# Grouped softmax on one core: ScalarE sums the last three tiles while it exponentiates them

## The chip, the cores and the metric

The kernel runs on one core of a Trainium2 chip. The metric is the device time of one execution in microseconds; lower is better. The kernel before takes 1326.22 us, the median of four runs (1325.66 to 1326.57).

## The reference

The input `x` is `[4, 4096, 4352]` in float32. Each row of 4352 numbers is cut into 8 groups of 544, and a softmax is taken over each group:

```python
x_g = x.reshape(B, N, G, Dg)                      # G = 8, Dg = 544
x_g = x_g - x_g.max(axis=-1, keepdims=True)
exp = np.exp(x_g)
out = exp / exp.sum(axis=-1, keepdims=True)
```

That makes 131,072 groups. 285.2 MB are read from HBM and as many written.

## The kernel before, in words

**Tiles.** The groups are seen as one list, and each of the 128 SBUF partitions works on 1024 of them. The list is cut into 57 tiles (`sizes`, line 34): 5, 11 and 15 groups per partition, then 51 tiles of `T = 19`, then 10, 9 and 5. A tile of 19 groups is 128 x 10336 floats, 5168 KB. Five buffers (`NT`) take turns: tile `t` lies in `xt` number `t % 5`. The last three tiles have `t` = 54, 55 and 56.

**The quick path.** The maximum is not subtracted. For each tile ScalarE takes the exponential in place, in one instruction for up to 19 groups (`scalar_tile`, line 88; tiles other than those of 19 groups are cut by `parts`, line 49, into pieces of at most `C = 10` groups). VectorE then sums each group (`reduce_sum`, line 102), takes the reciprocals (line 106) and multiplies the tile by them in place (line 109). `exp_done` counts ScalarE's pieces, `sum_done` and `rec_done` order VectorE's own steps, and `scaled` rises by one when a whole tile has been multiplied.

**The check and the slow path.** After the last tile `judge` (line 115) takes the largest and smallest of all sums on VectorE, tests them against 1e30 and 1e-6, adds up the answers over the partitions with a matmul, and writes a `verdict`. SP, ScalarE and VectorE load it (line 160) and branch. Only if a sum was out of bounds do they enter the loop from line 168, which computes everything again with the maximum subtracted. With this input they don't.

**Who moves the data.** SP issues all loads in order (line 137), each after the store that freed its buffer has landed. POOL issues the stores of all tiles but the last two (line 144). SP issues the stores of the last two tiles (line 140, `LAST = 2`), behind its loads. A store is issued when `scaled` has reached its tile. The profile calls SP's transfers q1 (hardware_dynamic) and POOL's q0 (software_dynamic); both run on the same 16 DMA engines.

**How the kernel ends.** The order in which POOL's queue ends is written out by hand:

```python
for t in range(nt - NT, nt - LAST):
    nc.gpsimd.wait_ge(stored[t % NT], 16 * (t // NT + 1))
nc.gpsimd.drain()
nc.gpsimd.wait_ge(last_stored, 16 * LAST)
```

POOL waits until its own last three stores, up to the 10-group tile, have landed. It then drains, waits until SP's two stores have landed, and goes on to the closing barrier of all engines.

Of the kernel before, what the change touches and what calls it, by code (L numbers as in the profile page):

```python
# [9 lines left out]
def kernel(  # L10
# [5 lines left out]
    nc = tc.nc  # L16
    G = 8
    P = 128
    NT = 5
    LAST = 2  # L20
    C = 10
    LOW, HIGH = 1e-6, 1e30
    f32 = mybir.dt.float32
    X = mybir.AxisListType.X
    Exp = mybir.ActivationFunctionType.Exp
    ET = mybir.EngineType
    op = mybir.AluOpType
# [3 lines left out]
    Dg = D // G  # L31
    per = N * G // P
    T = 19
    sizes = [5, 11, 15] + [T] * (per // T - 2) + [10, 9, 5]
    assert sum(sizes) == per
    nt = len(sizes)
    start = [sum(sizes[:t]) for t in range(nt + 1)]
# [9 lines left out]
        return a[lo:hi, :].rearrange("(p g) d -> p (g d)", p=P)  # L47

    def parts(t):
        size = T if sizes[t] == T else C  # L50
        return [(c, min(c + size, sizes[t])) for c in range(0, sizes[t], size)]

    before = [0]
    for t in range(nt):
        before.append(before[-1] + len(parts(t)))

    landed = [tc.alloc_semaphore(f"landed{b}") for b in range(NT)]
    stored = [tc.alloc_semaphore(f"stored{b}") for b in range(NT)]
    last_stored = tc.alloc_semaphore("last_stored")
    exp_done = tc.alloc_semaphore("exp_done")  # L60
    sum_done = tc.alloc_semaphore("sum_done")
    rec_done = tc.alloc_semaphore("rec_done")
    scaled = tc.alloc_semaphore("scaled")
    tested = tc.alloc_semaphore("tested")
# [4 lines left out]
    ctx.enter_context(tc.tile_critical(  # L69
        sync_engine=mybir.EngineType.Pool, no_gpsimd_drain=True))  # L70
    bufs = [ctx.enter_context(nc.sbuf_tensor(f"xt{b}", [P, T * Dg], f32)) for b in range(NT)]
    sums = ctx.enter_context(nc.sbuf_tensor("sums", [P, per], f32))
    rs = ctx.enter_context(nc.sbuf_tensor("rs", [P, NT, T], f32))
    mx = ctx.enter_context(nc.sbuf_tensor("mx", [P, R * G], f32))
    one = ctx.enter_context(nc.sbuf_tensor("one", [P, 1], f32))
    extreme = ctx.enter_context(nc.sbuf_tensor("extreme", [P, 2], f32))
    within = ctx.enter_context(nc.sbuf_tensor("within", [P, 2], f32))
    count = ctx.enter_context(nc.sbuf_tensor("count", [1, 1], f32))
    verdict = ctx.enter_context(nc.sbuf_tensor("verdict", [1, 1], mybir.dt.int32))
    found = ctx.enter_context(nc.psum_tensor("found", [1, 2], f32))  # L80

    def groups(b, lo, hi):
        return bufs[b][:, lo * Dg:hi * Dg].rearrange("p (g d) -> p g d", d=Dg)
# [4 lines left out]
    def scalar_tile(t):  # L88
        b = t % NT
        for k, (lo, hi) in enumerate(parts(t)):  # L90
            i = nc.scalar.activation(  # L91
                out=groups(b, lo, hi), in_=groups(b, lo, hi), func=Exp, scale=1.0)
            if k == 0:
                i.wait_op(landed[b], 16 * (t // NT + 1), "sem-ge")
            i.then_inc(exp_done, 1)

    def vector_tile(t):
        b = t % NT
        size = sizes[t]
        at = start[t]  # L100
        for k, (lo, hi) in enumerate(parts(t)):
            i = nc.vector.reduce_sum(  # L102
                out=sums[:, at + lo:at + hi], in_=groups(b, lo, hi), axis=X).wait_op(
                exp_done, before[t] + k + 1, "sem-ge")
        i.then_inc(sum_done, 1)
        nc.vector.reciprocal(out=rs[:, b, :size], in_=sums[:, at:at + size]).wait_op(  # L106
            sum_done, t + 1, "sem-ge").then_inc(rec_done, 1)
        xg = groups(b, 0, size)
        nc.vector.tensor_tensor(  # L109
            out=xg, in0=xg,  # L110
            in1=rs[:, b, :size].unsqueeze(2).to_broadcast([P, size, Dg]),
            op=op.mult,
        ).wait_op(rec_done, t + 1, "sem-ge").then_inc(scaled, 1)

    def judge():
        nc.vector.memset(one[:, :], 1.0).then_inc(tested, 1)  # L116
        for k, o in enumerate((op.max, op.min)):
            nc.vector.tensor_reduce(  # L118
                out=extreme[:, k:k + 1], in_=sums[:, :], axis=X, op=o).then_inc(tested, 1)
        nc.vector.wait_ge(tested, 3)  # L120
        for k, (o, limit) in enumerate(((op.is_le, HIGH), (op.is_ge, LOW))):
            nc.vector.tensor_scalar(  # L122
                out=within[:, k:k + 1], in0=extreme[:, k:k + 1], scalar1=limit, scalar2=None,
                op0=o).then_inc(tested, 1)
        nc.tensor.wait_ge(tested, 5)
        nc.tensor.matmul(  # L126
            out=found[:, :], lhsT=one[:, :], rhs=within[:, :],
            start=True, stop=True).then_inc(counted, 1)
        nc.vector.wait_ge(counted, 1)
        nc.vector.reduce_sum(out=count[:, :], in_=found[:, :], axis=X).then_inc(tested, 1)  # L130
        nc.vector.wait_ge(tested, 6)
        nc.vector.tensor_copy(out=verdict[:, :], in_=count[:, :]).then_inc(judged, 1)  # L132

    for t in range(nt):
# [16 lines left out]
    for t in range(nt):  # L151
        scalar_tile(t)

    for t in range(nt):
        vector_tile(t)
    judge()

    regs = nc.alloc_registers("verdict", [ET.SP, ET.Activation, ET.DVE])
    for e, reg in zip((nc.sync, nc.scalar, nc.vector), regs):
        e.reg_load(reg, verdict[0:1, 0:1]).wait_op(judged, 1, "sem-ge")  # L160
    with nc.If_cmp(regs, 2 * P, "IS_LT"):
        for t in range(nt - NT, nt - LAST):
            nc.sync.wait_ge(stored[t % NT], 16 * (t // NT + 1))
        nc.sync.wait_ge(last_stored, 16 * LAST)
        xb = bufs[0][:, :R * D]
        xg = groups(0, 0, R * G)
        sm, rg = sums[:, :R * G], rs[:, 0, :R * G]
        with nc.Fori(0, rows, engines=[ET.SP, ET.Activation, ET.DVE]) as t:
            nc.sync.dma_start(
                out=xb, in_=xr[bass.ds(t, 1)].rearrange("t p f -> (t p) f")).then_inc(again["in"], 16)  # L170
            nc.sync.wait_ge(again["out"], 1)
            nc.sync.sem_inc(again["out"], -1)
            nc.sync.dma_start(
                out=outr[bass.ds(t, 1)].rearrange("t p f -> (t p) f"), in_=xb).then_inc(again["end"], 16)
            nc.sync.wait_ge(again["end"], 16)
            nc.sync.sem_inc(again["end"], -16)

            nc.scalar.wait_ge(again["max"], 1)
            nc.scalar.sem_inc(again["max"], -1)
            for g in range(R * G):  # L180
                i = nc.scalar.activation(
                    out=xg[:, g, :], in_=xg[:, g, :], func=Exp,
                    bias=mx[:, g:g + 1], scale=1.0, accum_out=sm[:, g:g + 1])
            i.then_inc(again["exp"], 1)

            nc.vector.wait_ge(again["in"], 16)
            nc.vector.sem_inc(again["in"], -16)
            nc.vector.reduce_max(out=mx[:, :], in_=xg, axis=X, negate=True).then_inc(again["max"], 1)
            nc.vector.wait_ge(again["exp"], 1)
            nc.vector.sem_inc(again["exp"], -1)  # L190
            nc.vector.reciprocal(out=rg, in_=sm).then_inc(again["rec"], 1)
            nc.vector.wait_ge(again["rec"], 1)
            nc.vector.sem_inc(again["rec"], -1)
            nc.vector.tensor_tensor(
                out=xg, in0=xg, in1=rg.unsqueeze(2).to_broadcast([P, R * G, Dg]),
                op=op.mult).then_inc(again["out"], 1)
# [30 lines left out]
```

## Time and profile before

| | |
|---|---|
| median of four runs | 1326.22 us (1325.66 to 1326.57) |
| the profiled execution | 1326.17 us, with a span of 1324.4 us |
| VectorE busy | 1196.0 us (90%) |
| ScalarE busy | 477.3 us (36%) |
| DMA, mean over the span | 431 GB/s |
| exponential of 19 groups, ScalarE | 8.82 us |
| sums of 19 groups, VectorE | 10.92 us |
| multiply of 19 groups, VectorE | 10.93 us |
| start of one 19-group tile to the next, late in the run | 24.5 us |

The span is the time from the first to the last instruction of the core; some 1.8 us of the execution lie around it. The page of the profile gives the busy time of the engines first, then the busy share in 40 slices of 33.1 us each, then the DMA queues, then the chain of work that ended last, and then the groups of instructions by line with the mean time of one and the idle time ahead of them. Semaphore waits, branches and drains are not counted as busy; they are asked for by their line. Windows give the same busy times for any stretch, with the share of the 16 DMA engines that were busy and the GB/s as the last two columns.

### The profile page before, as it was taken

Reading aid. Unit: us, or ns where it says so; the run is one execution under the profiler, and the core shown is the slowest. Engines: PE = TensorE matmul, PEld = TensorE weight load, DVE = VectorE, ACT = ScalarE, POOL = GpSimd, SP = SyncE. Lnnn points to the kernel's source line nnn. Section 1 sums busy time; section 2 is a strip of 40 time slices with the busy share of each in tenths; the row PEclk is TensorE's granted clock in tenths of the full one; section 3 lists DMA queues with packets and bytes.
Section 4 is the critical chain, followed back from the end, with each engine's and each line's share of the span. In section 5 each row is a group of like instructions: output and inputs, shape, how many; then the busy total and the mean of one; then the engine's idle time right before and its main releaser. Section 6 shows DMA issues by size and latency. Waiting matters only on the chain.

```text
span 1324.4 us, 429 instructions
## 1 busy us (share of the span) xinstructions
PE 0.2 (0%) x2; PEld 0.1 (0%) x2; DVE 1196.0 (90%) x180; ACT 477.3 (36%) x60; POOL 29.6 (2%) x59
## 2 busy tenths in 40 slices
PE   0000000000000000000000000000000000000000
PEld 0000000000000000000000000000000000000000
DVE  6999899899899899898898998998998998989998
ACT  4342523423423324325225234234243243252331
POOL 0000000000000000000000000000000000000000
DMA  9999999999999999999999999999999999999998
GB/s 403 422 436 436 428 435 440 430 430 440 431 428 440 437 428 433 438 428 432 440 432 431 436 437 430 432 438 430 431 438 436 430 433 438 428 433 438 430 426 368
DMA packets 16421, 570.47 MB, mean 431 GB/s; under 512 B 1824, under 2 KB 1824, under 8 KB 1824
## 3 DMA queue, kind: packets, MB, share of 16 engines
q1 hardware_dynamic: 8496, 289.12, 50.6%
q0 software_dynamic: 7920, 281.32, 49.1%
q14 instruction: 5, 0.04, 0.0%
HBM read 285.21 MB, written 285.21 MB: 431 GB/s over the span
## 4 chain that ended last, share of the span: by engine, by line
another core or an unknown queue 56%; ACT 33%; DMA 6%; DVE 4%; issue 0%; PE 0%; POOLq 0%; SPq 0%
ACT xt L91 33%; DMA xt<-in_x_dram 4%; DVE xt L109 2%; DVE sums L102 2%; DMA out_dram<-xt 1%; DVE extreme L118 0%; DVE rs L106 0%; DVE within L122 0%; PE found L126 0%; DVE count L130 0%; DVE verdict L132 0%; SPq L222 0%; POOLq L69 0%; POOLq L211 0%
## 5 line engine op out<-in xcount | busy, mean ns | idle before, releaser
L91 ACT ACTIVATE xt<-xt 128x10336 f32<-128x10336 f32 (+4 forms) x59 | 476.0, 8071 | 827.9 <-DMA xt<-in_x_dram 827.9
L102 DVE TENSOR_REDUCE sums<-xt 128x19 f32<-128x10336 f32 (+4 forms) x59 | 589.1, 9987 | 119.2 <-ACT xt L91 119.2
L109 DVE TENSOR_TENSOR xt<-xt,rs 128x10336 f32<-128x10336 f32 (+5 forms) x57 | 589.3, 10339 | 2.0
L144 POOL DMA_DIRECT2D out_dram<-xt x55 | 29.4, 534 | 1270.5 <-DVE xt L109 1270.5
L106 DVE RECIPROCAL rs<-sums 128x19 f32<-128x19 f32 (+5 forms) x57 | 15.4, 270 | 2.0
L118 DVE TENSOR_REDUCE extreme<-sums 128x1 f32<-128x1024 f32 x2 | 2.3, 1214 | 0.0
L150 ACT ACT_TABLE_LOAD x1 | 1.3, 1283 | 0.9 <-PEq L211 0.9
L130 DVE TENSOR_REDUCE count<-found 1x1 f32<-1x2 f32 x1 | 0.1, 148 | 0.3 <-PE found L126 0.3
L126 PE MATMUL found<-within,one 128*1 128x2 f32 x2 | 0.2, 164 | 1318.9 <-DVE within L122 1318.9
L122 DVE TENSOR_SCALAR within<-extreme 128x1 f32<-128x1 f32 x2 | 0.2, 148 | 0.0
L132 DVE CAST verdict<-count 1x1 int32<-1x1 f32 x1 | 0.1, 142 | 0.0
L126 PEld LDWEIGHTS found<-within,one 128*1 128x1 f32 x2 | 0.1, 80 | 1318.9 <-DVE within L122 1318.9
L211 POOL MEMSET const-float32-0.0<- 128x1 f32 x1 | 0.1, 99 | 0.3 <-issue 0.3
L211 POOL MEMSET const-bfloat16-1.0<- 128x1 bf16 x1 | 0.1, 102 | 0.0
L211 POOL MEMSET const-float32-1.0<- 128x1 f32 x1 | 0.1, 99 | 0.0
L211 POOL MEMSET const-uint8-127<- 128x1 uint8 x1 | 0.1, 99 | 0.0
L116 DVE MEMSET one<- 128x1 f32 x1 | 0.1, 59 | 0.0
## 6 DMA issues: line engine op xcount, KB each, us to landing
xt<-in_x_dram SPq DMA_DIRECT2D x51, 5168.0 KB, 55.0
out_dram<-xt POOLq DMA_DIRECT2D x51, 5168.0 KB, 35.8
xt<-in_x_dram SPq DMA_DIRECT2D x1, 4080.0 KB, 23.5
out_dram<-xt POOLq DMA_DIRECT2D x1, 4080.0 KB, 27.8
xt<-in_x_dram SPq DMA_DIRECT2D x1, 2992.0 KB, 12.6
out_dram<-xt POOLq DMA_DIRECT2D x1, 2992.0 KB, 23.5
xt<-in_x_dram SPq DMA_DIRECT2D x2, 1360.0 KB, 19.5
xt<-in_x_dram SPq DMA_DIRECT2D x1, 2720.0 KB, 49.2
```

Of the source, the lines that this page charges most:

```text
L91: i = nc.scalar.activation(out=groups(b, lo, hi), in_=groups(b, lo, hi), func=Exp, scale=1.0)
L102: i = nc.vector.reduce_sum(out=sums[:, at + lo:at + hi], in_=groups(b, lo, hi), axis=X).wait_op(exp_done, before[t] + k + 1, "sem-ge")
L106: nc.vector.reciprocal(out=rs[:, b, :size], in_=sums[:, at:at + size]).wait_op(sum_done, t + 1, "sem-ge").then_inc(rec_done, 1)
L109: nc.vector.tensor_tensor(out=xg, in0=xg, in1=rs[:, b, :size].unsqueeze(2).to_broadcast([P, size, Dg]), op=op.mult,).wait_op(rec_done, t + ...
L116: nc.vector.memset(one[:, :], 1.0).then_inc(tested, 1)
L118: nc.vector.tensor_reduce(out=extreme[:, k:k + 1], in_=sums[:, :], axis=X, op=o).then_inc(tested, 1)
L122: nc.vector.tensor_scalar(out=within[:, k:k + 1], in0=extreme[:, k:k + 1], scalar1=limit, scalar2=None, op0=o).then_inc(tested, 1)
L126: nc.tensor.matmul(out=found[:, :], lhsT=one[:, :], rhs=within[:, :], start=True, stop=True).then_inc(counted, 1)
L130: nc.vector.reduce_sum(out=count[:, :], in_=found[:, :], axis=X).then_inc(tested, 1)
L144: nc.gpsimd.dma_start(out=dram(og_all, t), in_=buf(t)).then_inc(stored[t % NT], 16)
L150: nc.scalar.preload_act_table(Exp)
L211: nc = _bacc.Bacc("TRN2", target_bir_lowering=False, num_devices=1)
```

## The change

For the last three tiles (`SUMMED = 3`) ScalarE issues one exponential for each group, and each of them also writes the sum of its group (`accum_out`) into a new buffer `tail_sums`. These tiles are cut into parts of five groups (`FINE`): 5 + 5, 5 + 4 and 5. `exp_done` rises once for each part. VectorE no longer sums these tiles. For each part it waits for ScalarE's part, takes the reciprocals and multiplies. `scaled` still rises once for each tile, after its last part. Since the sums now lie in two buffers, `judge` takes four extremes instead of two, and tests them two at a time. All other tiles, the loads and the stores are written as before.

```diff
+    FINE = 5
...
+    SUMMED = 3
...
     def parts(t):
-        size = T if sizes[t] == T else C
+        size = FINE if t >= nt - SUMMED else T if sizes[t] == T else C
...
-            i = nc.scalar.activation(
-                out=groups(b, lo, hi), in_=groups(b, lo, hi), func=Exp, scale=1.0)
+            xg = groups(b, lo, hi)
+            if t < nt - SUMMED:
+                runs = [nc.scalar.activation(out=xg, in_=xg, func=Exp, scale=1.0)]
+            else:
+                runs = [
+                    nc.scalar.activation(
+                        out=xg[:, g - lo, :], in_=xg[:, g - lo, :], func=Exp, scale=1.0,
+                        accum_out=tail_sums[:, start[t] - summed + g:start[t] - summed + g + 1])
+                    for g in range(lo, hi)]
             if k == 0:
-                i.wait_op(landed[b], 16 * (t // NT + 1), "sem-ge")
-            i.then_inc(exp_done, 1)
+                runs[0].wait_op(landed[b], 16 * (t // NT + 1), "sem-ge")
+            runs[-1].then_inc(exp_done, 1)
...
+        for k, (lo, hi) in enumerate(whole if t < nt - SUMMED else parts(t)):
+            n = t + 1 if t < nt - SUMMED else nt - SUMMED + before[t] - before[nt - SUMMED] + k + 1
+            from_ = sums if t < nt - SUMMED else tail_sums
+            first = at if t < nt - SUMMED else at - summed
+            i = nc.vector.reciprocal(out=rs[:, b, lo:hi], in_=from_[:, first + lo:first + hi])
+            if t < nt - SUMMED:
+                i.wait_op(sum_done, n, "sem-ge")
+            else:
+                i.wait_op(exp_done, before[t] + k + 1, "sem-ge")
+            i.then_inc(rec_done, 1)
+            xg = groups(b, lo, hi)
+            i = nc.vector.tensor_tensor(
+                out=xg, in0=xg,
+                in1=rs[:, b, lo:hi].unsqueeze(2).to_broadcast([P, hi - lo, Dg]),
+                op=op.mult,
+            ).wait_op(rec_done, n, "sem-ge")
+        i.then_inc(scaled, 1)
...
+        for h, part in enumerate((sums, tail_sums)):
+            for k, o in enumerate((op.max, op.min)):
+                nc.vector.tensor_reduce(
+                    out=extreme[:, 2 * k + h:2 * k + h + 1], in_=part[:, :], axis=X,
+                    op=o).then_inc(tested, 1)
...
-    with nc.If_cmp(regs, 2 * P, "IS_LT"):
+    with nc.If_cmp(regs, 4 * P, "IS_LT"):
```

More of the change, by code (lines that the diff above doesn't have):

```diff
@@ L71 @@
     bufs = [ctx.enter_context(nc.sbuf_tensor(f"xt{b}", [P, T * Dg], f32)) for b in range(NT)]
-    sums = ctx.enter_context(nc.sbuf_tensor("sums", [P, per], f32))
+    summed = start[nt - SUMMED]
+    tail_sums = ctx.enter_context(nc.sbuf_tensor("tail_sums", [P, per - summed], f32))
+    sums = ctx.enter_context(nc.sbuf_tensor("sums", [P, summed], f32))
     rs = ctx.enter_context(nc.sbuf_tensor("rs", [P, NT, T], f32))
@@ L75 @@
     one = ctx.enter_context(nc.sbuf_tensor("one", [P, 1], f32))
-    extreme = ctx.enter_context(nc.sbuf_tensor("extreme", [P, 2], f32))
-    within = ctx.enter_context(nc.sbuf_tensor("within", [P, 2], f32))
+    extreme = ctx.enter_context(nc.sbuf_tensor("extreme", [P, 4], f32))
+    within = ctx.enter_context(nc.sbuf_tensor("within", [P, 4], f32))
     count = ctx.enter_context(nc.sbuf_tensor("count", [1, 1], f32))
     verdict = ctx.enter_context(nc.sbuf_tensor("verdict", [1, 1], mybir.dt.int32))
-    found = ctx.enter_context(nc.psum_tensor("found", [1, 2], f32))
+    found = ctx.enter_context(nc.psum_tensor("found", [1, 4], f32))
     def groups(b, lo, hi):
@@ L100, in vector_tile @@
         at = start[t]
[L101 to L113, printed above, removed]
+        whole = [(0, size)]
@@ new lines, in vector_tile @@
+        if t < nt - SUMMED:
+            for k, (lo, hi) in enumerate(parts(t)):
+                i = nc.vector.reduce_sum(
+                    out=sums[:, at + lo:at + hi], in_=groups(b, lo, hi), axis=X).wait_op(
+                    exp_done, before[t] + k + 1, "sem-ge")
+            i.then_inc(sum_done, 1)
+        for k, (lo, hi) in enumerate(whole if t < nt - SUMMED else parts(t)):
[3 more added lines that the diff above has]
+            i = nc.vector.reciprocal(out=rs[:, b, lo:hi], in_=from_[:, first + lo:first + hi])
+            if t < nt - SUMMED:
+                i.wait_op(sum_done, n, "sem-ge")
[8 more added lines that the diff above has]
+            ).wait_op(rec_done, n, "sem-ge")
@@ L115, in judge @@
+        i.then_inc(scaled, 1)
     def judge():
         nc.vector.memset(one[:, :], 1.0).then_inc(tested, 1)
[L117 to L120, printed above, removed]
+        for h, part in enumerate((sums, tail_sums)):
[3 more added lines that the diff above has]
+                    op=o).then_inc(tested, 1)
@@ L121, in judge @@
+        nc.vector.wait_ge(tested, 5)
         for k, (o, limit) in enumerate(((op.is_le, HIGH), (op.is_ge, LOW))):
             nc.vector.tensor_scalar(
-                out=within[:, k:k + 1], in0=extreme[:, k:k + 1], scalar1=limit, scalar2=None,
-                op0=o).then_inc(tested, 1)
-        nc.tensor.wait_ge(tested, 5)
+                out=within[:, 2 * k:2 * k + 2], in0=extreme[:, 2 * k:2 * k + 2],
+                scalar1=limit, scalar2=None, op0=o).then_inc(tested, 1)
+        nc.tensor.wait_ge(tested, 7)
@@ L130, in judge @@
         nc.vector.reduce_sum(out=count[:, :], in_=found[:, :], axis=X).then_inc(tested, 1)
-        nc.vector.wait_ge(tested, 6)
+        nc.vector.wait_ge(tested, 8)
         nc.vector.tensor_copy(out=verdict[:, :], in_=count[:, :]).then_inc(judged, 1)
```

## The prediction

> **What bounds the kernel now.** I read the page first, then the DMA windows of the last 16 us, then the timeline of the end, and last the sequencer instructions of the end. Call the last three tiles A (10 groups), B (9) and C (5), and the 19-group tile before them T.
>
> ```profile
> span 1324.4 us, 429 instructions
> PE 0.2 (0%) x2; PEld 0.1 (0%) x2; DVE 1196.0 (90%) x180; ACT 477.3 (36%) x60; POOL 29.6 (2%) x59
> DMA  9999999999999999999999999999999999999998
> q1 hardware_dynamic: 8496, 289.12, 50.6%
> q0 software_dynamic: 7920, 281.32, 49.1%
> ```
>
> VectorE is busy 90%, but the DMA row is at 9 in all slices but the last, and the two queues fill 99.7% of sixteen engines' span. q1 carries the loads and the stores of B and C (SP), q0 all other stores (POOL). VectorE's 90% is the second limit, not the first.
>
> ```profile
> 1306.00:1308.00 2.00, 0.00 (x0) 0.00 (x0) 2.00 (x1) 0.13 (x1) 0.00 (x0) 1.00 0.99 424
> 1308.00:1310.00 2.00, 0.00 (x0) 0.00 (x0) 2.00 (x1) 0.00 (x0) 0.00 (x0) 1.00 1.04 446
> 1310.00:1312.00 2.00, 0.00 (x0) 0.00 (x0) 2.00 (x2) 0.00 (x0) 0.00 (x0) 1.00 0.80 337
> 1312.00:1314.00 2.00, 0.00 (x0) 0.00 (x0) 1.93 (x3) 0.00 (x0) 0.00 (x0) 1.00 0.74 313
> 1314.00:1316.00 2.00, 0.00 (x0) 0.00 (x0) 2.00 (x1) 0.00 (x0) 0.00 (x0) 1.00 1.09 470
> 1316.00:1318.00 2.00, 0.00 (x0) 0.00 (x0) 2.00 (x4) 0.00 (x0) 0.00 (x0) 1.00 0.80 339
> 1318.00:1320.00 2.00, 0.19 (x2) 0.09 (x2) 1.13 (x5) 0.00 (x0) 0.00 (x0) 1.00 1.02 430
> ```
>
> The last two columns are the DMA share and GB/s. VectorE works almost without a pause to 1319.5 us and the chain of waits runs along it, which suggests that each microsecond off VectorE is a microsecond gained. But the DMA engines starve only a little: the unfilled shares of these rows, the two above 1 counted against them, come to 2 x (0.20 + 0.26 + 0.20 - 0.09 - 0.02 - 0.04 + 0.01) = 1.0 us. That is nearly all that earlier stores can win back.
>
> ```profile
> 1299.80 0.53 POOL L144 DMA_DIRECT2D out_dram<-xt  x1 [11.31 <-DVE xt L109]
> 1303.66 2.47 ACT L91 ACTIVATE xt<-xt 128x2720 f32<-128x2720 f32 x1 [8.55 <-DMA xt<-in_x_dram]
> 1310.24 6.49 SPq L140 DMA_DIRECT2D out_dram<-xt  x2
> 1313.36 2.99 DVE L109 TENSOR_TENSOR xt<-xt,rs 128x2720 f32<-128x2720 f32 x1
> ```
>
> POOL issues A's store at 1299.80, SP B's at 1310.24 and C's at 1316.38; C's data landed at 1303.6. The issue table gives 13.4, 8.8 and 6.3 us to landing: A lands at 1313.2, B at 1319.0, C at 1322.7.
>
> ```profile
> L147 POOLq DRAIN  x1: 4552/4552/4552, 1313.3 to 1313.3; - x1
> ...
> L137 POOLq COMPARE_BRANCH  x1: 33/33/33, 1322.7 to 1322.7; - x1
> ```
>
> These are POOL's last steps: once A's store, the last on its own queue, has landed, it drains for 4.55 us (1313.31 to 1317.86), then waits for C's landing, branches at 1322.69, and 1.7 us of closing barriers follow. Today the drain ends 4.8 us before it is needed.
>
> I also read the trace's packet records one by one. Packets of 41,344 B (T) take 1.53 us on an engine, 21,760 B (A) 0.81, 19,584 B (B) 0.73, 10,880 B (C) 0.41. One of the sixteen engines is late. It runs without a gap from 1292 to 1321.86, while the others starve briefly at 1311 and 1317 and still end at 1320.6. C's store lands on fifteen engines at 1320.9 to 1321.0 and on the late one at 1322.67. Each landing counts when the sixteenth is in, so the late engine alone sets the end, and its work doesn't shrink.
>
> **What the Trainium skill says.** "DMA: Bandwidth & Descriptors", section "Queues, rings and completion order": an engine takes turns between the queues that have work, a packet at a time. The records agree: from 1292 to 1302 the late engine alternates one T store packet (1.53 us) with one C load packet (0.41 us). The same page, "Latency and other measured facts", says that some DMA engines are usually slower; the trace has one, 1.7 us late at the end. "PSUM — Partial Sum Buffer", section "Engine vs sequencer instructions": a drain waits for its engine to go fully idle. It gives no price; the trace has 4.55 us. "ScalarE: Activation LUTs", section "What ACT_TABLE_LOAD costs": 186 ns plus 0.833 ns per element, 93 ns less back to back; the 128x544 ACTIVATE took 640 ns and the 128x10336 one 8817, which agrees.
>
> **The change, part by part.**
>
> *ScalarE.* 24 one-group ACTIVATEs with sums replace three large ones (4.74 + 4.28 + 2.47 us). No row has a summing ACTIVATE, and the pages price none. Lower end 0.55 us (640 ns less the overlap), upper 0.95 (640 ns and as much again as a small VectorE instruction, 0.19 to 0.28, for reading out the sum). I take 0.75. A: 1275.3 + 7.5 = 1282.8, hidden under VectorE's work on T until 1287.6. B landed at 1290.8: first five groups at 1294.6, all at 1297.6. C landed at 1303.65: 1307.4.
>
> *VectorE.* Reductions of 5.81 + 5.24 + 2.98 = 14.0 us go; each part costs a reciprocal (0.22 with its gap) and a multiply (2.99 for five groups, about 2.4 for four). A: 1287.6 + 2 x 3.2 = 1294.05, before 1299.5. B: 1294.6 + 3.2 = 1297.8, then 2.6 more, 1300.45, before 1310.2. C: 1307.45 + 3.2 = 1310.65, before 1316.35. The new wait of part two on ScalarE (at most 0.2 us at 0.75 per group) has only that tile's multiply behind it. At 0.95 C ends at 1311.65, still early.
>
> *The verdict.* Two short reductions more, 0.15 to 0.3 us each by the small rows: about 0.4. It is done near 1314.2 instead of 1319.5, and its loads (0.86 us) and branches near 1315.1. POOL's later end hides it; without that cover it would still have C's transfer over it. The branches cause 8 KB instruction fetches (today at 1321.6 and 1321.9, 0.37 to 0.49 us), which would now run under the stores: nothing, or 0.4 us if one meets the late engine. Semaphore and buffer edits cost nothing: no instruction is added to SP or POOL.
>
> *The stores.* A's issue moves to 1294.3, B's to 1300.5, C's to 1310.7. A only joins the queue behind T, which is unchanged. B and C are on q1, which had been empty while A was written. Now B's packets take turns with T's and A's. On the late engine, from 1301.8: q0 still has three T packets (4.6) and eight of A (6.5), 11.1 us. Ten turns of q1 fall between the eleven: the load's semaphore (nothing), B's eight (5.8) and one of C (0.4). One more C packet goes ahead of A's semaphore write. A is written at 1301.8 + 11.1 + 6.2 + 0.4 = 1319.5 instead of 1312.8. C still ends at 1321.9, since the sum of the bytes is the same.
>
> *POOL.* A lands 0.4 later, 1319.9; 0.12 to the drain's start, as before; plus 4.55: 1324.57; the branch at 1324.6 instead of 1322.69. So the end goes 1.9 us **later**: a wait on A through the drain takes the place of the wait on C. The drain's cost is the term that the trace shows only once. Lower end 0.2 us (the longest other POOL drain is 0.18), upper 5; I take 4.55, since POOL had nothing running when it began, so what it paid looks fixed.
>
> **The sum.** The profiled run took 1326.17 us (span 1324.4, 1.8 around it), 0.05 below the median of 1326.22. 1326.17 + 1.9 = 1328.1 us, 0.14% above the median. About 0.2% (2.65 us) is what a measurement of this kernel can tell from no change; I forecast a small loss inside it. With a fetch on the late engine and with a different order of turns around A, it is 1327.3 to 1329.0.
>
> **Rivals.**
> 1. *The drain is not in the way* (it is shorter when the core is quiet: VectorE's multiply ran from 1313.36 to 1316.35 beside it, and if that held it up, 1.5 us remain). Then it ends by 1321.6 and C's landing sets the end as today: 1326.1. For it: the drain shows up once, beside that multiply. Against it: it outlasts the multiply by 1.5 us, and does not end with any VectorE instruction.
> 2. *VectorE's gain arrives*: the late engine is not late in an ordinary run, the 1.0 us of holes closes, and the drain is covered: 1325.1. For it: the chain of waits runs along VectorE. Against it: that engine's unbroken row. More than this isn't there to be won, whatever VectorE saves.
> 3. *Slower beyond 0.2%*: q1 gets more than every other turn, so that A's packets come last with C's. A lands at 1322.3, the drain ends at 1326.95, the branch moves by 4.3: 1330.5. It decides from a landing of A after 1320.6, 0.7 us beyond my estimate. For it: C's packets are short, and a fetch adds 0.4. Against it: the one-to-one turns of 1292 to 1302.
>
> **Chances.** Forecast 0.64 (of which 0.06 over the 0.2% line), rival 1 0.18, rival 2 0.08, rival 3 0.10. Slower by over 0.2%: 0.10 + 0.06 = 0.16; faster by over 0.2%: 0.03, out of rival 2 if holes before 1306 closed too; within: 0.81. The range runs from below rival 1 to the upper end of the forecast, 1325.6 to 1329.2, and leaves out rival 3 and most of rival 2.
>
> **What would show it.** VectorE's last multiply ends near 1310.7 and B's store is issued near 1300.5; ACTIVATE rows of 544 near 0.75 us. A's store takes about 25 us to landing instead of 13.4. The drain starts near 1320 and the branch follows its end directly. The forecast is wrong if the drain takes well under 4 us, if A lands before 1318, or if C's landing is still what POOL waits for last.

## The result, and the profile after

The changed kernel takes 1328.74 us (median of 38 runs), the kernel before 1326.05 us in runs beside it (58 runs). The ratio is 1.0020, with a 95% interval of 1.0015 to 1.0025: slower by 2.0 to 3.3 us. The profiled execution took 1329.40 us, its span is 1327.6 us; before they were 1326.17 and 1324.4.

The top of the page of the changed kernel:

```profile
span 1327.6 us, 477 instructions
PE 0.2 (0%) x2; PEld 0.1 (0%) x2; DVE 1182.7 (89%) x183; ACT 481.5 (36%) x105; POOL 29.7 (2%) x59
DMA  9999999999999999999999999999999999999997
```

VectorE did lose 13.3 us of work, and the span is 3.2 us longer all the same. The DMA row is full as before, except for its last slice, which went from 8 to 7: the end now has more time in which no data move. The timeline of the changed kernel at the end:

```profile
1294.50 0.53 POOL L168 DMA_DIRECT2D out_dram<-xt  x1 [5.72 <-DVE xt L130]
...
1300.27 10.74 SPq L164 DMA_DIRECT2D out_dram<-xt  x2
1304.09 0.66 ACT L100 ACTIVATE xt<-xt 128x544 f32<-128x544 f32 x1 [7.09 <-DMA xt<-in_x_dram]
...
1307.65 2.99 DVE L130 TENSOR_TENSOR xt<-xt,rs 128x2720 f32<-128x2720 f32 x1
```

The stores are early: A's is issued at 1294.5 (before 1299.8), B's at 1300.27 (1310.24), C's at 1310.67 (1316.38). Now the transfers from 1285 us on, with the time from issue to landing as the last column:

```profile
out_dram<-xt POOLq DMA_DIRECT2D x1, 5168.0 KB, 20.4
out_dram<-xt POOLq DMA_DIRECT2D x1, 2720.0 KB, 26.7
out_dram<-xt SPq DMA_DIRECT2D x1, 2448.0 KB, 17.7
out_dram<-xt SPq DMA_DIRECT2D x1, 1360.0 KB, 12.7
```

The last three in the kernel before:

```profile
out_dram<-xt POOLq DMA_DIRECT2D x1, 2720.0 KB, 13.4
out_dram<-xt SPq DMA_DIRECT2D x1, 2448.0 KB, 8.8
out_dram<-xt SPq DMA_DIRECT2D x1, 1360.0 KB, 6.3
```

Each takes twice as long as before, because they now share the engines. A is issued 5.3 us earlier and lands at 1321.2, 8.0 us **later** than before. B lands at 1317.9 (1.1 earlier), C at 1323.4 (0.7 later). POOL's last steps in the changed kernel:

```profile
L171 POOLq DRAIN  x1: 4552/4552/4552, 1321.3 to 1321.3; - x1
```

```profile
L161 POOLq COMPARE_BRANCH  x1: 33/33/33, 1325.9 to 1325.9; - x1
```

The drain runs from 1321.32 to 1325.87 and the branch follows at 1325.92, 2.5 us after the last data landed. Before, the same branch stood at 1322.69, right behind C's landing. The difference of the two, 3.2 us, is the whole difference of the spans. The windows say the same from the side of the DMA engines (share and GB/s are the last two columns):

```profile
1318.00:1320.00 2.00, 0.00 (x0) 0.00 (x0) 0.00 (x0) 0.00 (x0) 0.00 (x0) 1.00 0.66 275
1320.00:1322.00 2.00, 0.00 (x0) 0.00 (x0) 0.00 (x0) 0.00 (x0) 0.00 (x0) 1.00 0.07 27
1322.00:1324.00 2.00, 0.00 (x0) 0.00 (x0) 0.00 (x0) 0.00 (x0) 0.00 (x0) 1.00 0.03 11
```

Fourteen engines have done their share of the last store by 1320.1, one by 1321.0 and the late one by 1323.4. From 1320 on nearly nothing moves, and the kernel lasts 7 us more.

### The profile page after: what moved, and what is told of

Its sections match the earlier page's. It is cut to its first block, busy times and chain, and to the rows that moved or that the text cites. A ratio compares the mean times of both kernels' runs of the same rounds, so it can differ in the third digit from the quotient of the medians.

```text
span 1327.6 us, 477 instructions
## 1 busy us (share of the span) xinstructions
PE 0.2 (0%) x2; PEld 0.1 (0%) x2; DVE 1182.7 (89%) x183; ACT 481.5 (36%) x105; POOL 29.7 (2%) x59
## 4 chain that ended last, share of the span: by engine, by line
another core or an unknown queue 54%; ACT 32%; DMA 10%; DVE 3%; issue 0%; PE 0%; POOLq 0%; SPq 0%
ACT xt L97 31%; DMA xt<-in_x_dram 7%; DMA out_dram<-xt 4%; DVE xt L130 1%; DVE sums L115 1%; ACT xt L100 0%; DVE extreme L141 0%; DVE rs L123 0%; DVE within L146 0%; PE found L150 0%; DVE count L154 0%; DVE verdict L156 0%; SPq L246 0%; POOLq L71 0%
## 5 line engine op out<-in xcount | busy, mean ns | idle before, releaser
L97 ACT ACTIVATE xt<-xt 128x10336 f32<-128x10336 f32 (+3 forms) x56 | 464.5, 8298 | 799.0 <-DMA xt<-in_x_dram 799.0
L115 DVE TENSOR_REDUCE sums<-xt 128x19 f32<-128x10336 f32 (+3 forms) x56 | 575.1, 10272 | 119.5 <-ACT xt L97 119.5
L130 DVE TENSOR_TENSOR xt<-xt,rs 128x10336 f32<-128x10336 f32 (+4 forms) x59 | 589.6, 9994 | 2.0
L100 ACT ACTIVATE xt<-xt 128x544 f32<-128x544 f32 x24 | 15.4, 644 | 26.0 <-DMA xt<-in_x_dram 26.0
L123 DVE RECIPROCAL rs<-sums 128x19 f32<-128x19 f32 (+3 forms) x54 | 14.8, 273 | 1.8
L100 ACT ACTIVATION_READ_ACCUMULATOR xt<-xt 128x1 f32 x24 | 4.5, 189 | 0.0
```

The source lines that it names most:

```text
L97: runs = [nc.scalar.activation(out=xg, in_=xg, func=Exp, scale=1.0)]
L100: nc.scalar.activation(out=xg[:, g - lo, :], in_=xg[:, g - lo, :], func=Exp, scale=1.0, accum_out=tail_sums[:, start[t] - summed + g:start ...
L115: i = nc.vector.reduce_sum(out=sums[:, at + lo:at + hi], in_=groups(b, lo, hi), axis=X).wait_op(exp_done, before[t] + k + 1, "sem-ge")
L123: i = nc.vector.reciprocal(out=rs[:, b, lo:hi], in_=from_[:, first + lo:first + hi])
L130: i = nc.vector.tensor_tensor(out=xg, in0=xg, in1=rs[:, b, lo:hi].unsqueeze(2).to_broadcast([P, hi - lo, Dg]), op=op.mult,).wait_op(rec_do ...
```

## The experiments

The theory is "drain behind A": the earlier store of B slows A's store down, and the drain, which stands behind the wait for A, ends after the last landing. Rival "instructions": the added instructions or the longer check cost the time. Rival "transfers": stores that share the engines land later as a whole. Each measured ratio is against the kernel before on the same chip, with its 95% interval.

### The instructions without the order: b_held

```diff
     for t in range(nt - LAST, nt):
-        nc.sync.wait_ge(scaled, t + 1)
+        nc.sync.wait_ge(scaled, nt)
```

> The changed kernel, but SP issues B's store only when C has been multiplied too, near 1310.7, so that A has the engines to itself as before. Drain behind A: A lands near 1313 to 1314, the drain is over by 1318.5, 1326.1 us with all of the changed computation kept. Transfers: also 1326.1, since the stores no longer mix. Instructions: 1328.7.

Measured: 1326.35 us, ratio 1.0000 (0.9992 to 1.0009). B's and C's stores are issued at 1308.6 and 1309.0 (C had loaded 2 us sooner than in the changed kernel), A lands at 1313.9, the drain is over at 1318.5, and the branch waits for C's landing at 1322.84:

```profile
L171 POOLq DRAIN  x1: 4552/4552/4552, 1314.0 to 1314.0; - x1
```

```profile
L161 POOLq COMPARE_BRANCH  x1: 33/33/33, 1322.9 to 1322.9; - x1
```

All of the changed computation is there and the loss is gone. The rival "instructions" falls.

### The order without the instructions: before_no_tail_sums2

```diff
-        for k, (lo, hi) in enumerate(parts(t)):
-            i = nc.vector.reduce_sum(
...
+        if t < nt - 3:
+            for k, (lo, hi) in enumerate(parts(t)):
+                i = nc.vector.reduce_sum(
...
+        else:
+            nc.vector.reciprocal(out=rs[:, b, :size], in_=sums[:, :size]).wait_op(
+                exp_done, before[t + 1], "sem-ge").then_inc(rec_done, 1)
```

The extremes are taken over the sums that are still written.

> The kernel before, which leaves out the sums of the last three tiles and scales these by the reciprocals of the first tiles' sums instead: VectorE is as early as in the changed kernel, with nothing added on ScalarE and the small check as before. Drain behind A: B is issued near 1300.6, A lands near 1321, 1328.7 us. Instructions (the summing ACTIVATEs or the longer check cost the time): 1326.1.

Measured: 1328.40 us, ratio 1.0016 (1.0009 to 1.0022). A lands at 1320.4, and its drain ends last:

```profile
L151 POOLq DRAIN  x1: 4552/4552/4552, 1320.5 to 1320.5; - x1
```

The loss is there without one summing ACTIVATE. What costs the time is that VectorE is early, not how it got there.

### A taken out of the drain's way: a_on_sp

```diff
-    LAST = 2
+    LAST = 3
```

> The changed kernel with A's store moved from POOL to SP (LAST = 3), so that POOL's drain waits only for T's landing near 1308. Theory 'drain behind A': the drain is over near 1313, C's landing sets the end again, 1326.1 us. Rival 'transfers': stores that take turns on the engines land later by themselves, and the time stays near 1328.7. Rival 'instructions': the added ScalarE and VectorE work costs the time, also 1328.7.

Measured: 1326.68 us, ratio 1.0003 (0.9995 to 1.0012). The profiled execution took 1324.93 us, one of the shortest of the 13. The drain begins when T has landed:

```profile
L171 POOLq DRAIN  x1: 4476/4476/4476, 1309.9 to 1309.9; - x1
```

It is over at 1314.4, and C's landing at 1321.3 sets the end. The three stores are issued no later than in the changed kernel (1294.7, 1300.3 and 1303.5), so early stores alone don't cost time that these runs could show, and they don't gain any either. This run also changes the order of the packets: A, B and C now stand one behind the other on SP's queue, and A lands at 1312.3. So it takes the drain off A, but it doesn't keep A late. What bounds the rival "transfers" is the changed kernel itself: there the last landing is 0.7 us later than before, the end 3.2, and the branch follows the end of the drain within 0.05 us. At most those 0.7 us are left to "transfers".

### Without the drain: no_drain

```diff
-    nc.gpsimd.drain()
     nc.gpsimd.wait_ge(last_stored, 16 * LAST)
```

> The changed kernel without POOL's drain; all waits on landings stay, and all stores are issued as in the changed kernel. Drain behind A: 1326.1 us, the last landing sets the end. Transfers: 1328.7, since the order of the packets is the same. Instructions: 1328.7.

Measured: 1331.11 us, ratio 1.0036 (1.0022 to 1.0050), **slower** than the changed kernel (all five runs took over 1330.9 us, 37 of the 38 of the changed kernel under 1329.7), which no theory had expected. POOL leaves its last wait at 1323.2, as I had thought, but then comes the closing barrier (line 245 of this kernel). Of its three drains on POOL the first, at 1324.06, is the long one; the columns are the shortest, the median and the longest in ns:

```profile
L245 POOLq DRAIN  x3: 34/113/4552, 1324.1 to 1329.2; - x3
```

In the kernel before and the changed one the same three take 0.03 to 0.11 us. So the price of 4.55 us isn't that of the line which I took away. Whatever drain comes first after POOL's stores pays it; the written one only decides where it is paid. My theory was right about the drain's place and wrong in that it could be left out.

### The drain's price in a quiet core: before_drain_last

```diff
-    nc.gpsimd.drain()
     nc.gpsimd.wait_ge(last_stored, 16 * LAST)
+    nc.gpsimd.drain()
```

> The kernel before with the drain after the wait for SP's two stores instead of ahead of it. If the drain has a fixed price of 4.55 us wherever it stands, the end moves by 4.6 to 4.7: 1330.7 us. If it is short while the other engines are quiet (1.5 us), 1327.6.

Measured: 1330.62 us, ratio 1.0033 (1.0020 to 1.0045).

```profile
L148 POOLq DRAIN  x1: 4557/4557/4557, 1322.6 to 1322.6; - x1
```

Here nothing else runs, no multiply and no store, and A had landed 9.6 us before, where it was 0.1 in the kernel before. The drain takes 4.557 us instead of 4.552. So it neither gets shorter in a quiet core nor waits for POOL's last store to settle. The price is fixed in these runs, and it is paid in full when nothing lies over it.

### Less of the change: summed_1 and summed_2

```diff
-    SUMMED = 3
+    SUMMED = 1        # summed_2: SUMMED = 2
```

> The changed kernel with SUMMED = 1: only the last tile (C) is summed on ScalarE, so C's store is issued near 1313.4 while A's and B's stay at 1299.8 and 1310.2. Drain behind A: A lands near 1313 as before and the drain is covered: 1326.1 us. If it were the added instructions or the larger check that cost time, 1327 or more.

> The changed kernel with SUMMED = 2: B and C are summed on ScalarE. A is issued near 1299.5 as before, B near 1305.3 instead of 1310.2, so B takes turns with all of A but not with T. Drain behind A: A lands near 1319.2, the drain ends near 1323.9, 1.2 us after the old branch: 1327.3 us, between the kernel before and the changed one. If the loss came from T's store being disturbed, 1326.1.

summed_1 measured: 1326.62 us, ratio 1.0004 (0.9995 to 1.0012). Only C is early, A lands at 1313.2 and the drain is covered, as expected. summed_2 measured: 1326.81 us, ratio 1.0001 (0.9992 to 1.0009), where I had expected 1327.3. B was issued at 1305.43, but A landed at 1318.2, 1 us sooner than I had worked out, so the drain was over at 1322.9, just ahead of C's landing at 1323.6:

```profile
L171 POOLq DRAIN  x1: 4552/4552/4552, 1318.3 to 1318.3; - x1
```

```profile
L161 POOLq COMPARE_BRANCH  x1: 33/33/33, 1323.6 to 1323.6; - x1
```

So the loss does not grow evenly with the share of the change. It begins where A's landing plus 4.67 us (0.12 to the drain's start, 4.55 for it) passes C's landing.

### Why A lands later than I had worked out: verdict_late2

```diff
         nc.vector.reduce_sum(out=count[:, :], in_=found[:, :], axis=X).then_inc(tested, 1)
+        nc.vector.wait_ge(last_stored, 16 * LAST)
         nc.vector.wait_ge(tested, 8)
```

> The changed kernel with one wait more: VectorE writes the verdict only after SP's two stores have landed, so that the three branches and the instruction fetches that they cause come after all stores. If the fetches on the late engine are what made A land 1.3 us later than I had worked out, A lands near 1320.0 to 1320.3 instead of 1321.2, the drain still ends last, and the time falls by about 1 us to 1327.7. If they don't matter: 1328.7, with A at 1321.2.

The packet records don't name the engines; I followed the late one by packets that join without a gap. In the changed kernel it finishes A's data at 1319.44, moves one packet of C, then an instruction fetch of 8 KB (1319.84, 0.37 us), and only then writes A's semaphore, at 1320.19, which counts at 1321.20. I put the fetches down to the branches at 1315.1. With the branches moved behind the stores there is no fetch in the last 40 us before 1324.2, and A lands at 1319.99. The trace of no_drain repeats the picture: a fetch of 0.35 us ends just before A's semaphore is written at 1319.77, and that counts 1.1 us later, at 1320.89. In before_no_tail_sums2 no fetch stands there; the semaphore counts 0.5 us after its write, and A lands at 1320.41. Measured: 1328.14 us, ratio 1.0016 (1.0007 to 1.0024). The profiled execution fell by 1.2 us, from 1329.40 to 1328.19. A's landing is as expected; that the time follows is likely, but the two intervals overlap, so it is not shown.

### POOL without transfers: before_act_stores and after_act_stores

```diff
-    for t in range(nt - LAST):
-        nc.gpsimd.wait_ge(scaled, t + 1)
-        nc.gpsimd.dma_start(out=dram(og_all, t), in_=buf(t)).then_inc(stored[t % NT], 16)
...
-    nc.gpsimd.drain()
...
     for t in range(nt):
         scalar_tile(t)
+        if 1 <= t <= nt - LAST:
+            nc.scalar.wait_ge(scaled, t)
+            nc.scalar.dma_start(out=dram(og_all, t - 1), in_=buf(t - 1)).then_inc(stored[(t - 1) % NT], 16)
```

> The kernel before with POOL's stores issued by ScalarE instead, each after the exponential of the next tile; POOL issues no transfer and its explicit drain is left out, so the first drain on POOL is the one of the closing barrier. If the 4.55 us belong to POOL having issued transfers, that drain is short and the end follows the last landing: 1326.1 us, or about 1324.8 if the late DMA engine also goes with POOL's queue. If the first drain always costs 4.55 us: 1330.5.

> The changed kernel with the same move of POOL's stores to ScalarE and no explicit drain. With no drain in the way the time is that of the last landing. If the late engine still sets it: 1326.1 us, no gain from the change. If the late engine goes with POOL's queue, the change wins back the holes of about 1.0 us on top: near 1323.8. If the first drain on POOL always costs 4.55 us: 1330.5.

Measured: from the kernel before 1325.41 us, ratio 0.9994 (0.9987 to 1.0000); from the changed kernel 1325.30 us, ratio 0.9993 (0.9986 to 0.9999). Both are at or under the kernel before, and they can't be told apart. The closing barrier of before_act_stores (line 221), whose first drain is now POOL's first:

```profile
L221 POOLq DRAIN  x3: 34/41/99, 1322.4 to 1323.1; - x3
```

Without transfers of its own POOL drains in 0.1 us at most. The price of 4.55 us belongs to a POOL that has issued transfers.

In before_act_stores no engine is late at the end: the last store lands on all sixteen between 1321.60 and 1321.78. That doesn't mean that the late engines went with POOL's queue. At 1269.6 the sixteenth engine still finished its part of a 19-group store 1.7 us after the first; in the kernel before it was 1.6 us (at 1270.6). The engines even out later. VectorE does bound the end here, as these windows show, in which the engines starve while B's and C's stores wait for it:

```profile
1310.00:1312.00 2.00, 0.00 (x0) 0.00 (x0) 2.00 (x2) 0.00 (x0) 0.00 (x0) 1.00 0.42 178
1312.00:1314.00 2.00, 0.00 (x0) 0.00 (x0) 1.97 (x2) 0.00 (x0) 0.00 (x0) 1.00 0.75 313
```

The same windows of after_act_stores:

```profile
1310.00:1312.00 2.00, 0.00 (x0) 0.00 (x0) 0.00 (x0) 0.00 (x0) 0.00 (x0) 1.00 1.03 443
1312.00:1314.00 2.00, 0.00 (x0) 0.00 (x0) 0.00 (x0) 0.00 (x0) 0.00 (x0) 1.00 1.02 421
```

The change fills these holes, and the spread stays. Thirteen engines then have the last store done by 1319.9, two microseconds sooner, but three are done at 1321.2, 1321.5 and 1321.8. The landing counts with the last of them, so the gain is lost once more. The expected 1323.8 was wrong for that reason. Why three engines are late there, two of them by 5 us when C's load landed at 1297.8, stays open.

## Why the prediction was right, and where it was off

**VectorE is not the bound: right.** 13.3 us went from it and no time was won, with the drain in the way (the changed kernel) or out of it (a_on_sp, 1.0003).

**ScalarE and VectorE: right.** I took 0.75 us for a summing group. From start to start the groups take 0.64. The sum's read-out, 189 ns, starts 0.1 us before the next exponential and ends 0.1 us after that has started. What such a group takes without the sum, back to back, no run shows; the lower end of the prediction was 0.55. The by-shape rows of the changed kernel:

```profile
L100 ACT ACTIVATE xt<-xt 128x544 f32<-128x544 f32 x24 | 15.4, 644 | 26.0 <-DMA xt<-in_x_dram 26.0
L100 ACT ACTIVATION_READ_ACCUMULATOR xt<-xt 128x1 f32 x24 | 4.5, 189 | 0.0
```

The last multiply ended at 1310.64 (forecast 1310.65). That it fits so closely is luck: C's load landed 0.4 us later than in the kernel before, and its five groups took 0.5 us less than forecast. The stores were issued within 0.3 us of the forecast.

**The longer check: right about the instructions, not about what follows them.** From the first extreme to the verdict it took 3.34 us instead of 3.20, 0.14 more where I had put 0.4, and all of it was hidden, as b_held shows. The fetches behind the branches I had put at nothing, or 0.4 us if one met the late engine. One did, and A's semaphore counted 1.0 us after it was written instead of 0.4.

**The drain takes over from C's landing: right.** It took 4.552 us, as before. Rival 1, a shorter drain in a quiet core, falls with before_drain_last (4.557 us). Rival 2, VectorE's gain arriving, falls with a_on_sp. Rival 3, A coming last of all, did not happen: A landed 2.2 us before C, and the late engine kept its one-to-one turns. But the mark set for it, a landing of A after 1320.6, was passed in the profile (1321.2), and the profiled pair lies 0.24% apart: the forecast mechanism alone, with a later A, was enough for that.

**The holes.** The sum of 1.0 us is right, but three of its rows lie above a share of 1 and are counted against the others, not two.

**The size: too small.** I forecast a loss of 1.9 us; the runs give 2.65 (2.0 to 3.3), the profiled pair 3.2. The term that was mis-sized is A's landing: 1319.9 forecast, 1321.2 in the profile. The late engine finished A's data about 0.3 us later than worked out, since it ran 0.3 us further behind already when B had loaded, before the change begins to act. The rest, about 1 us, is the fetch (0.37) and the slow count of A's semaphore (1.0 instead of 0.4). Without the fetches A landed at 1319.99. So the time came out on the 0.2% line, where I had given most of the chance to the inside of it.

## What to carry to other kernels

Where the DMA engines have hardly any free time, as here, a faster compute engine may do no more than change the order in which transfers finish. List what waits for each transfer that becomes later, above all steps of fixed price behind it, such as a drain, and compare their ends with the last landing. A step that is hidden today has a margin (here 4.8 us): price the change against that margin and not against the busy time that it saves.

## What the runs showed of the hardware that was not expected

- The first drain on POOL after it has issued transfers takes 4.55 us (4.476 to 4.557 in ten kernels), whether the core is busy or quiet, and whether POOL's last store landed 0.1 or 9.6 us before. If it is taken out of the program, the closing barrier's first drain takes 4.552 us instead. With the transfers issued by ScalarE the drains take 0.03 to 0.10 us.
- The DMA engines don't finish together, and a landing counts with the last. In the kernel before it is one engine: A's store counts there 1.90 us after the fifteenth, the last store 1.66. "DMA: Bandwidth & Descriptors", section "Latency and other measured facts", has a best guess that ties slow engines to POOL's descriptor rings. These runs don't bear it out: with ScalarE issuing POOL's stores the changed kernel has three late engines (the last store counts 1.3 to 1.8 us after the thirteenth).
- Instruction fetches of 8 KB run on the same DMA engines, and those of the end follow the branches. In the changed kernel they started 4.0 and 4.8 us after the first branch, for 0.31 and 0.37 us, and one stood ahead of the semaphore that POOL waited for. With the branches at 1323.1 (verdict_late2) the first came at 1324.2.
